# A two-layer hybrid block: norm weights spread by a product, a second layer's first weights split earlier, later transposes, another order at the end

## The chip, the cores and the metric

One core of a Trainium2 chip runs the kernel. It has five engines with their own instruction queues: TensorE (PE; its weight loads are PEld), VectorE (DVE), ScalarE (ACT), GpSimd (POOL) and SyncE (SP), which here issues transfers between HBM (DRAM) and the on-chip memory (SBUF). TensorE writes its sums to a second memory, PSUM. The metric is the device time of one execution in microseconds (us); the median of three runs is compared. The profile's span goes from the first to the last instruction of one execution.

## The reference

A sequence of 512 tokens with 1024 channels goes through two layers and a last norm. Each layer normalises, projects to the inputs of three mixers (an RWKV-7 recurrence, a gated linear recurrence, a latent attention of 8 heads), gates their outputs and adds their projection to the residual h.

```python
def rms_norm(x, g, eps=NORM_EPS):
    xf = x.astype(jnp.float32)
    y = xf * lax.rsqrt(jnp.mean(xf * xf, axis=-1, keepdims=True) + eps)
    return (y * g.astype(jnp.float32)).astype(x.dtype)

    h = x
    for l in range(DEPTH):
        xn = rms_norm(h, ln_g[l])
        proj = xn @ w_in[l]
        u_a, z_a, u_b, z_b, q_lat, kv_lat, k_rope, z_c = jnp.split(proj, pts, axis=-1)
        y_a = rwkv7_mix(u_a, ...)
        y_b = rms_norm(rglru_mix(u_b, ...), lru_out_g[l])
        y_c = rms_norm(mla_mix(q_lat, kv_lat, k_rope, ...), mla_out_g[l])
        y = jnp.concatenate([y_a * silu(z_a), y_b * silu(z_b), y_c * silu(z_c)], axis=-1)
        h = h + y @ w_out[l]
    return rms_norm(h, final_g)
```

The change touches the norms at the start of each layer, the first projections, and the last norm; not the mixers' arithmetic.

## The kernel before

**Tiling.** Tokens stand in four tiles of 128 (`tt` 0 to 3), channels in halves of 512 (`n`) or blocks of 128. The normalised input is kept transposed, channels on the partitions, as a pair: `xH`, rounded to the fast f32 form of TensorE, and `xL`, the rest. Weights are split likewise: `weights` (L216) loads a raw half of 128x512 into one of three buffers `wr`, ScalarE rounds it into one of four `wH` (L141, the line of every plain copy), and VectorE or POOL subtracts for `wL` (L229). A product takes three matmuls (`mm3`, L233 to L235): high by high, high by low, low by high.

**The opening.** SyncE's queue loads x tile by tile (L158), the identity, the norm weights broadcast to 128 partitions (`gb0`, L173), and the first raw weights, in the order of the string `LO` ("0ig12uw3yvcm": digits are tiles of x, i the identity, g the norm weights, u and w the two halves of projection 12, y the first half of projection 0). For each tile `h_half` squares and sums two halves on ScalarE (L242), `h_rstd` makes the scale (VectorE L246, a logarithm and an exponential on ScalarE L138, VectorE L254 to L256), and `norm_tile` scales the tile by it and the norm weights (VectorE L298), transposes blocks of 128 on TensorE (L303) and splits them into `xH` (ScalarE L141) and `xL` (VectorE L306). Two PSUM buffers `ps` take the transposes. `behind` and `BN` hold certain weight copies on ScalarE behind the copies of a tile.

**A layer.** `one_layer` starts with projection 12 and projection 0, each in two halves of tokens (`halves=True`), so the first half needs tiles 0 and 1 only, the second tiles 2 and 3. Then come the other projections and the three mixers, in orders written out as strings. The attention's last step is `heads(3, ...)` (L1067 on): per block of keys it transposes the probabilities (L1076), copies them (L141), and multiplies them with the values (L1084), with products of the first output projection (`units`) in between.

**The passage to the next layer.** `out_proj(2, ..., True)` adds the attention's part of the output projection. For channel half `n` = 1 it works tile after tile: residual load `hp` (L446), 12 matmuls, `finish`. `finish` adds the residual (VectorE L461), writes h back (L464), squares (L242), multiplies with the norm weights (`norm_gain`, L286, POOL for n = 0, VectorE for n = 1), and at n = 1 calls `norm_tile`, which there scales what `norm_gain` left (L301), transposes and splits. After the second layer it calls `final_tile` instead: scale, VectorE for n = 1 (L316), ScalarE for n = 0 (L141), and one transfer out for each half (L319), from SyncE's and ScalarE's queues.

**Order.** The source gives each engine's instructions in program order; the builder then puts them into each engine's queue, so the order in a trace isn't that of the source. `tc.issue_after(i)` keeps the instructions of a block behind `i` on `i`'s engine.

## Time and profile before

| | us |
|---|---|
| median of three runs (849.64 to 851.14) | 849.87 |
| the profiled execution | 847.71 |
| its span | 845.9 |
| TensorE busy in the span | 791.7 |
| VectorE, ScalarE, POOL busy | 538.9, 519.3, 353.3 |

Mean granted TensorE clock: 0.984. The span begins with loads; TensorE's first instruction starts at 9.28 us, the first product of a projection at 15.87. Layer two's first product starts at 430.31, the last product of the kernel at 836.81.

How to read the rows below. A row of the order of time has the start, the duration, engine, line, operation, output tile <- input tiles, the shape, xN for N merged instructions, and in brackets the engine's idle time before it with what ended it. A row of a stretch has start:end, its length, the busy time of PE, PEld, DVE, ACT and POOL with instruction counts, the granted clock (1.00 is full), the DMA engines' busy share, and GB/s. SPq and ACTq are transfers being issued. A row of the transfers has what is loaded, the queue, the count, the size and the median us from issue to landing.

### The profile page before, as it was taken

How to read it: one execution, taken by the hardware profiler on the slowest of the kernel's cores; microseconds unless marked ns; L12 is line 12 of the kernel's file. 1: busy time of each engine (PE TensorE's matmuls, PEld its weight loads, DVE VectorE, ACT ScalarE, POOL GpSimd, SP SyncE). 2: the span in 40 equal slices, each digit the busy share in tenths (PEclk: the TensorE clock that was granted, in tenths of full speed). 3: DMA queues.
4: the chain of work that ended last, by engine and by line, in shares of the span. 5: the costliest groups of instructions: out<-in, count | busy, mean ns of one | idle time of the engine just before them, and what ended most of it. 6: DMA issues, size and time to landing. Idle time of an engine off the chain costs nothing. (4 is left out here: it accounts for less than half of the span.)

```text
span 845.9 us, 15219 instructions
## 1 busy us (share of the span) xinstructions
PE 791.7 (94%) x5696; PEld 619.4 (73%) x5696; DVE 538.9 (64%) x1115; ACT 519.3 (61%) x1018; POOL 353.3 (42%) x321
## 2 busy tenths in 40 slices
PE   4999999999879999999989999999998799999995
PEld 3878888886659877657778788888765697775674
DVE  5678776924977364774474966695367953577636
ACT  5667875657563576664467687845666436765635
POOL 0455557522452455022344556574143425530323
PEclk9999999999998999999999999999999899999998
DMA  7222134311113375123732233332001234731354
GB/s 246 98 76 74 66 111 132 112 58 33 33 39 113 120 229 193 55 90 92 272 122 89 75 100 100 101 112 92 30 26 43 80 95 140 244 120 50 112 174 162
DMA packets 49754, 91.07 MB, mean 108 GB/s; under 512 B 5520, under 2 KB 8336, under 8 KB 49680
## 3 DMA queue, kind: packets, MB, share of 16 engines
q1 hardware_dynamic: 49104, 89.05, 32.8%
q8 instruction: 45, 0.74, 0.4%
q10 hardware_dynamic: 576, 1.05, 0.3%
q14 instruction: 29, 0.24, 0.1%
HBM read 73.30 MB, written 16.78 MB: 106 GB/s over the span
## 5 line engine op out<-in xcount | busy, mean ns | idle before, releaser
L229 POOL TENSOR_TENSOR wL<-wr,wH 128x512 fp32r<-128x512 f32 (+1 forms) x148 | 196.8, 1336 | 283.9 <-ACT wH L141 270.4
L141 ACT ACTIVATE wH<-wr 128x512 fp32r<-128x512 f32 (+1 forms) x192 | 118.8, 622 | 142.8 <-PE acc L234 73.9
L233 PE MATMUL acc<-xH,wH 128*128 128x512 f32 (+1 forms) x496 | 191.9, 388 | 0.0
L234 PE MATMUL acc<-xL,wH 128*128 128x512 f32 (+1 forms) x496 | 189.3, 382 | 0.7 <-DVE xL L306 0.6
L235 PE MATMUL acc<-xH,wL 128*128 128x512 f32 (+1 forms) x496 | 188.5, 380 | 0.0
L234 PEld LDWEIGHTS acc<-xL,wH 128*128 128x128 f32 x496 | 94.0, 190 | 17.5 <-DVE xL L306 1.4
L233 PEld LDWEIGHTS acc<-xH,wH 128*128 128x128 f32 x496 | 93.5, 189 | 18.1 <-ACT xH L141 0.7
L235 PEld LDWEIGHTS acc<-xH,wL 128*128 128x128 f32 x496 | 93.9, 189 | 17.2
L233 PE MATMUL acc<-wH,c 128*128 128x512 f32 x192 | 82.5, 430 | 0.1
L234 PE MATMUL acc<-wL,c 128*128 128x512 f32 x192 | 76.7, 399 | 0.0
L235 PE MATMUL acc<-wH,c 128*128 128x512 f32 x192 | 76.2, 397 | 0.0
L141 ACT ACTIVATE UV<-ps 64x512 f32<-64x512 f32 (+4 forms) x112 | 52.4, 494 | 28.8 <-PE ps L1076 22.0
L229 DVE TENSOR_TENSOR wL<-wr,wH 128x512 fp32r<-128x512 f32 (+1 forms) x44 | 32.6, 744 | 53.0 <-ACT wH L141 52.9
L138 ACT ACTIVATE c<-acc,sm 128x128 f32<-128x128 f32 (+3 forms) x64 | 33.6, 528 | 19.0 <-DVE sm L1060 19.0
L1058 PE MATMUL acc<-am,am 128*128 128x128 f32 (+3 forms) x128 | 42.8, 447 | 0.9 <-ACT c L138 0.8
L234 PEld LDWEIGHTS acc<-wL,c 128*128 128x128 f32 x192 | 36.5, 190 | 8.7 <-issue 1.9
L233 PEld LDWEIGHTS acc<-wH,c 128*128 128x128 f32 x192 | 36.3, 189 | 8.7 <-issue 2.2
L235 PEld LDWEIGHTS acc<-wH,c 128*128 128x128 f32 x192 | 36.3, 189 | 8.2 <-issue 0.5
L136 ACT ACT_TABLE_LOAD x31 | 39.8, 1283 | 1.3 <-PEq L1215 0.7
L138 ACT ACTIVATE g<-g 128x512 f32<-128x512 f32 (+1 forms) x58 | 36.4, 628 | 4.6 <-DVE g L705 2.6
L369 POOL TENSOR_TENSOR g<-g,g 128x512 f32<-128x512 f32 x24 | 32.2, 1340 | 13.9 <-ACT g L138 13.9
L141 ACT ACTIVATE c<-g 128x512 fp32r<-128x512 f32 (+1 forms) x40 | 24.9, 629 | 18.8 <-DVE g L980 7.2
(219 smaller groups left out, 1587.7 us busy)
## 6 DMA issues: line engine op xcount, KB each, us to landing
wr<-in_wc_dram SPq DMA_DIRECT2D x116, 256.0 KB, 2.7
wr<-in_wo_dram SPq DMA_DIRECT2D x48, 256.0 KB, 3.4
hp<-dr SPq DMA_DIRECT2D x38, 256.0 KB, 3.5
dr<-hp SPq DMA_DIRECT2D x28, 256.0 KB, 3.3
dr<-g SPq DMA_DIRECT2D x16, 256.0 KB, 2.5
g<-dr SPq DMA_DIRECT2D x16, 256.0 KB, 3.5
wr<-in_wl_dram SPq DMA_DIRECT2D x16, 208.0 KB, 2.5
dr<-c SPq DMA_DIRECT2D x12, 256.0 KB, 3.7
```

Of the source, the lines that this page charges most:

```text
L136: chained(A.preload_act_table_set(SETS[st]))
L138: chained(A.activation(out=out, in_=in_, func=func, **kw))
L141: i = A.activation(out=out, in_=in_, func=AF.Copy, **kw)
L229: (V if wn[0] % wmod[0] == 0 or wn[0] <= 4 else G).tensor_tensor(out=L, in0=raw, in1=f(H), op=ALU.subtract)
L233: PE.matmul(o, a[0], b[0], start=start, stop=False)
L234: PE.matmul(o, a[0], b[1], start=False, stop=False)
L235: PE.matmul(o, a[1], b[0], start=False, stop=stop)
L369: G.tensor_tensor(out=z, in0=z, in1=s, op=ALU.mult)
L1058: PE.matmul(o[:, 0:n], qT[:, hd, qt * 128:n], K2[:, p, e, 0:n], start=True, stop=True)
```

## The change

Four places are edited.

1. **Opening.** The identity and the norm weights are loaded from ScalarE's queue, the norm weights as a single row on one partition. Two matmuls with a row of ones (`on1`) spread this row over 128 partitions into the two PSUM banks `ck` (`go`), and the scaling reads its factor there. SyncE's order becomes 0, u, w, 1, 2, y, 3, v, c, m, kept by `issue_after(queued)`, with the small later loads (`w2a2`, `gagx`) behind it. `keep_warm` issues 3, 5 and 3 matmuls (128 x 256, plain f32, result unused) behind the two spreading matmuls and behind the transposes of tiles 0 and 1. The two halves of projection 12 are split right behind tile 0's steps (`wfirst`).
2. **Attention's last step of layer one.** `first_weights(1)` loads and splits the four halves of layer two's projections 12 and 0 there, into a tile of the tag `am` (two buffers, shared with the attention's keys and queries), subtracting on POOL. `proj` then takes them from `wfirst`.
3. **Passage between the layers.** `norm_tile` is divided into `norm_scale` (at each tile's `finish`) and `norm_transposes`; the transposes of tiles 0 and 1 are issued after `finish` of tiles 2 and 3, those of 2 and 3 at the end.
4. **End.** ScalarE's scalings of the last norm go behind the table-ordered activation issued last; tile 3's second half is scaled and multiplied by the norm weights in one VectorE step; the first half of tile 2 is scaled and written after tile 3's.

```diff
-    BN = (2, 2, 0, 0)
+    BN = (0, 2, 0, 0)
-    LO = "0ig12uw3yvcm"
+    LO = "gi0uw12y3vcm"
-    raws, gb0 = {}, c4([128, D])
+    raws, gb0, on1 = {}, c4([128, D]), g2([1, 128])
+    G.memset(on1, 1.0)
-        "i": lambda: nc.sync.dma_start(out=C[:, 0:128], in_=cst[:, 0:128]),
+        "i": lambda: nc.scalar.dma_start(out=C[:, 0:128], in_=cst[:, 0:128]),
-        "g": lambda: nc.sync.dma_start(out=gb0, in_=ln_g[0].partition_broadcast(128)),
+        "g": lambda: nc.scalar.dma_start(out=gb0[0:1, :], in_=ln_g[0].unsqueeze(0)),
+    queued = None
     for t in LO:
-        x_load(int(t)) if t.isdigit() else loads[t]()
+        with (tc.issue_after(queued) if queued is not None and t not in "gi" else nullcontext()):
+            i = x_load(int(t)) if t.isdigit() else loads[t]()
+        if t not in "gi":
+            queued = getattr(i, "ins", i)
...
+            scaled[0] = V.scalar_tensor_tensor(out=src, in0=h[tt][:, s], scalar=rs, in1=gb[j], op0=ALU.mult, op1=ALU.mult).ins
             for k in range(4):
-                PE.transpose(p[:, k, :], src[:, k * 128:(k + 1) * 128], ident)
+                warmed[0] = PE.transpose(p[:, k, :], src[:, k * 128:(k + 1) * 128], ident).ins
...
+    def keep_warm(o, n):
+        w = smask.rearrange("p c s -> p (c s)")
+        with tc.issue_after(warmed[0]):
+            for _ in range(n):
+                i = PE.matmul(o, w[:, 0:128], w[:, 0:256], start=True, stop=True).ins
+        warmed[0] = i
...
+    def norm_scale(tt):
+        rs = h_rstd(tt)
+        for j in range(2):
+            V.tensor_scalar(out=hg[tt, j], in0=hg[tt, j], scalar1=rs, scalar2=None, op0=ALU.mult)
+
+    def norm_transposes(l, tt):
+        xH, xL, _ = xn[l]
+        c = slice(tt * 128, (tt + 1) * 128)
+        for j in range(2):
+            p = ps([128, 4, 128])
+            for k in range(4):
+                PE.transpose(p[:, k, :], hg[tt, j][:, k * 128:(k + 1) * 128], ident)
+            xh = xH[:, 4 * j:4 * j + 4, c]
+            copy(xh, p)
+            V.tensor_tensor(out=xL[:, 4 * j:4 * j + 4, c], in0=p, in1=f(xh), op=ALU.subtract)
+
+    def first_weights(l):
+        W = tl("am", [128, 4, 2, 512], F32R, bufs=2)
+        for i, (j, hf) in enumerate(((12, 0), (12, 1), (0, 0), (0, 1))):
+            raw = tl("wr", [128, 512], F32, bufs=3)
+            nc.sync.dma_start(out=raw, in_=wc[l, j, :, 4 * hf:4 * hf + 4, :].rearrange("p k c -> p (k c)"))
+            split(raw, W[:, i, 0, :], W[:, i, 1, :], G)
+            wfirst[j, hf] = W[:, i, 0, :], W[:, i, 1, :]
...
     def final_tile(tt):
-        rs = h_rstd(tt)
-        for n in range(2):
-            y = hg[tt, n]
-            if n:
+        fin[tt] = rs = h_rstd(tt)
+        for t, n in {2: ((2, 1),), 3: ((3, 1), (3, 0), (2, 0))}.get(tt, ((tt, 0), (tt, 1))):
+            y = hg[t, n] if (t, n) != (3, 1) else g2()
+            if (t, n) == (3, 1):
+                V.scalar_tensor_tensor(out=y, in0=h[t][:, 512:1024], scalar=rs, in1=xn[depth][2][:, 512:1024], op0=ALU.mult, op1=ALU.mult)
+            elif n:
                 V.tensor_scalar(out=y, in0=y, scalar1=rs, scalar2=None, op0=ALU.mult)
             else:
-                copy(y, y, scale=rs)
+                with tc.issue_after(last[0]):
+                    copy(y, y, scale=fin[t])
...
-                            norm_tile(l + 1, tt) if l + 1 < depth else final_tile(tt)
+                            norm_scale(tt) if l + 1 < depth else final_tile(tt)
...
                         finish(tt)
+                        if tt >= 2 and l + 1 < depth:
+                            norm_transposes(l + 1, tt - 2)
+                    if l + 1 < depth:
+                        for tt in (2, 3):
+                            norm_transposes(l + 1, tt)
...
             if p < 3:
                 ahead += score_steps(p + 1)
+            elif l + 1 < depth:
+                first_weights(l + 1)
             heads(p, [lambda t=t: emit(t) for t in s.split(",")])
...
-    norm_start(0, gb0)
+    go, wk = [ck(), ck()], acc([128, 256])
+    for n in range(2):
+        warmed[0] = PE.matmul(go[n], on1, gb0[0:1, n * 512:(n + 1) * 512], start=True, stop=True).ins
+    norm_start(0, go)
+    keep_warm(wk, 3)
     for tt in range(4):
...
-        last_v = norm_tile(0, tt)
+        last_v = norm_first(tt)
+        if tt < 2:
+            keep_warm(wk, (5, 3)[tt])
+        if tt == 0:
+            behind += [last[0]] * 2
+            with tc.issue_after(scaled[0]):
+                wfirst.update({(12, hf): weights(None, raw=raws.pop((12, hf))) for hf in range(2)})
```

## The prediction

> **What bounds the kernel now.** I read the page's totals first, then the order of time at three places (the opening, the passage between the layers, the end), because the diff touches only these and the last attention step.

> ```profile
> span 845.9 us, 15219 instructions
> PE 791.7 (94%) x5696; PEld 619.4 (73%) x5696; DVE 538.9 (64%) x1115; ACT 519.3 (61%) x1018; POOL 353.3 (42%) x321
> ...
> 25.24:115.00 89.76, 87.92 (x470) 72.70 (x471) 63.20 (x78) 65.15 (x108) 48.25 (x53) 1.00 0.28 89
> ```

> TensorE is busy 94% of the span, and for the 90 us behind the opening 87.92 of 89.76 us. So a stretch in which it waits, if shortened, moves everything behind it forward by that much; work moved on another engine inside a full stretch moves nothing. The profiled execution took 847.71 us, 1.8 us around its span; the median of the three timed runs is 849.87. I work out differences on the profiled execution and take them from the median.

> The opening, in order of time, and its stretches (the five engines' busy times, clock, DMA share, GB/s):

> ```profile
> 3.46 0.63 ACT L242 ACTIVATE g<-c 128x512 f32<-128x512 f32 x1 [1.44 <-DMA c<-in_x_dram]
> ...
> 5.92 0.16 DVE L256 SCALAR_TENSOR_TENSOR sm<-sm,sm 128x1 f32<-128x1 f32 x1
> ...
> 8.47 1.42 DVE L298 SCALAR_TENSOR_TENSOR g<-c,sm,c 128x512 f32<-128x512 f32 x2 [2.39 <-DMA c<-in_ln_g_dram]
> ...
> 9.02 0.63 ACT L242 ACTIVATE g<-c 128x512 f32<-128x512 f32 x1 [3.52 <-DMA c<-in_x_dram]
> ...
> 12.60 0.69 DVE L229 TENSOR_TENSOR wL<-wr,wH 128x512 fp32r<-128x512 f32 x1
> ...
> 13.20 1.41 DVE L298 SCALAR_TENSOR_TENSOR g<-c,sm,c 128x512 f32<-128x512 f32 x2
> ...
> 14.10 1.94 PE L303 MATMUL ps<-C,g 128*128 128x128 f32 x8 [2.85 <-DVE g L298]
> ...
> 15.87 0.58 PE L233 MATMUL acc<-xH,wH 128*128 128x256 f32 x1
> ...
> 20.54 0.60 PE L303 MATMUL ps<-C,g 128*128 128x128 f32 x4
> ...
> 25.24 0.50 PE L233 MATMUL acc<-xH,wH 128*128 128x256 f32 x2
> ...
> 0.00:4.00 4.00, 0.00 (x0) 0.00 (x0) 0.00 (x0) 1.82 (x3) 0.93 (x10) 1.00 0.58 154
> 4.00:6.00 2.00, 0.00 (x0) 0.00 (x0) 0.56 (x4) 1.24 (x6) 0.00 (x0) 1.00 0.71 152
> 6.00:8.00 2.00, 0.00 (x0) 0.00 (x0) 0.08 (x1) 0.00 (x0) 0.00 (x0) 1.00 0.95 329
> 8.00:10.00 2.00, 0.72 (x4) 0.72 (x5) 1.42 (x2) 0.98 (x3) 0.00 (x0) 1.00 1.05 392
> ```

> Tile 0 of x is there at 3.46 and its scale at 6.08, but the scaling (L298) waits 2.39 us for the broadcast norm weights; tile 1 of x comes at 9.02, after ScalarE stood 3.52 us. While the broadcast is under way, from 4 to 6 us, the DMA moves only 152 GB/s at a share of 0.71. The first product waits for tiles 0 and 1 (15.87), the second half of that projection for tiles 2 and 3 (25.24). The opening is bound by its loads, then by the chain of norm steps on VectorE and ScalarE.

> **The opening, part by part.** The broadcast (512 KB) becomes one row of 4 KB, and leaves SyncE's queue with the identity; two products of one row spread it into PSUM. In the queue tile 1 of x now stands behind tile 0 and two weight halves: 0.52 + 0.26 + 0.26 + 0.52 = 1.57 MB, 1.64 with identity and row. Up to 4 us the DMA moved 0.62 MB (154 GB/s × 4 us); the other 1.02 MB at 329 GB/s take 3.1 us. Tile 1 lands at about 7.1 instead of 9.02, **−1.9**, and at the 392 GB/s that the next stretch reached, −2.4; I take −2.1. Tile 0's scaling can begin at 6.1 (−2.4) if the row is spread by then. That product is not in the trace. The row is issued first and x itself, issued at 0.74, was in use at 3.46, so it is there at 3.5 to 4.5. Half-clock products of 512 columns are seen between the layers:

> ```profile
> 426.24 0.63 PE L235 MATMUL acc<-wH,c 128*128 128x512 f32 x1
> ...
> 426.66 0.62 PE L233 MATMUL acc<-wH,c 128*128 128x512 f32 x1
> ...
> 390.89 1.72 PE L1084 MATMUL ck<-UV 128*64 128x512 f32 x8
> ```

> They start 0.42 us apart. Plain f32 takes two passes (the eight instructions of the L1084 row are four products of the source), so two rows take 4 × 0.42 = 1.7 us, and the three warming products of 256 columns 6 × 0.21 = 1.3: TensorE is done at 6.5 to 7.5, and the first transposes want it at 6.8. At most 0.7 us is lost there. At best it costs nothing.

> The scaling reads PSUM now; the nearest row of that kind (L461, quoted below) takes 0.75 for one half against 1.42 / 2 = 0.71: 8 × 0.04 = **+0.3**. The warming products cost nothing: they stand where TensorE idles (2.85 us before 14.10), at worst 0.7 us ahead of the first product, which then still ends before tile 3 is ready. They should make the second tile's eight transposes 2 × 0.60 instead of 1.94; the first half of that is on the chain, **−0.3**. The first weights' split is put right behind tile 0's scaling, so the 0.69 us at 12.60 no longer stands ahead of tile 1's scaling: **−0.7**; it is 0 if it only comes in tile 0's way. The copies stand behind tile 0's exponential on ScalarE, in its former gap. No other VectorE work is taken from tiles 2 and 3, so the gain is carried as it is to tile 3 and the product at 25.24: −2.1 + 0.3 − 0.3 − 0.7 = **−2.8**, bounds −0.7 and −4.0.

> **Between the layers.** Stretches, then TensorE, VectorE, POOL and SyncE's queue:

> ```profile
> 421.50:431.20 9.70, 5.32 (x25) 4.12 (x24) 9.51 (x21) 6.52 (x17) 5.13 (x6) 0.82 0.44 159
> ...
> 424.04 1.97 PE L303 MATMUL ps<-C,g 128*128 128x128 f32 x8 [2.49 <-DVE g L301]
> ...
> 428.77 0.66 PE L303 MATMUL ps<-C,g 128*128 128x128 f32 x4 [1.01 <-DVE xL L306]
> ...
> 429.93 0.63 PE L303 MATMUL ps<-C,g 128*128 128x128 f32 x4 [0.51 <-DVE sm L254]
> ...
> 431.17 0.39 PE L234 MATMUL acc<-xL,wH 128*128 128x256 f32 x1 [0.37 <-DVE xL L306]
> ...
> 418.53 0.75 DVE L461 SCALAR_TENSOR_TENSOR c<-acc,sm,hp 128x512 f32<-128x512 f32 x1 [1.84 <-DMA hp<-dr]
> ...
> 424.30 1.27 DVE L254 TENSOR_TENSOR sm<-sm 128x1 f32<-128x1 f32 x1
> ...
> 426.09 1.24 DVE L255 SCALAR_TENSOR_TENSOR sm<-sm,sm 128x1 f32<-128x1 f32 x1
> ...
> 434.22 0.16 DVE L255 SCALAR_TENSOR_TENSOR sm<-sm,sm 128x1 f32<-128x1 f32 x1
> ...
> 423.93 3.38 POOL L229 TENSOR_TENSOR wL<-wr,wH 128x512 fp32r<-128x512 f32 x2
> ...
> 409.74 2.45 SPq L221 DMA_DIRECT2D wr<-in_wc_dram  x2
> ```

> Here 2.49 + 1.01 + 0.51 + 0.37 = 4.4 us of TensorE are idle, and the clock is 0.82. But VectorE is busy 9.51 of 9.70 us: it is the bound, from a late load of the residual (418.53) on. The diff takes no instruction from VectorE here. Moving transposes later in the program does little by itself: tile 0's transposes already stand in the source right behind tile 0's products and yet ran at 424.04, behind most of tile 3's, so the order on an engine goes by what is ready when it is built, and they are ready no sooner. The four split weight halves do go, but three buffers for raw weights and four for split ones then hold the next four: the loads at 409.74 and the POOL splits at 423.93 come back under another name, and SyncE's queue and its waits stay. I take **0**, bounds +1.5 (the second half of the split of x, L306, now ranks behind tile 3's steps) and −4.4.

> The splits' new place, the last attention step:

> ```profile
> 385.00:390.00 5.00, 5.00 (x34) 3.86 (x34) 1.94 (x3) 3.33 (x8) 1.29 (x1) 1.00 0.31 105
> ...
> 393.08 0.66 ACT L141 ACTIVATE UV<-ps 128x256 f32<-128x256 f32 x2 [3.54 <-PE ps L1076]
> ...
> 397.00 3.00 POOL L229 TENSOR_TENSOR wL<-wr,wH 128x512 fp32r<-128x512 f32 x2 [8.43 <-ACT wH L141]
> ...
> wr<-in_wo_dram SPq DMA_DIRECT2D x6, 256.0 KB, 4.2
> ```

> Four copies of 0.63 as at 3.46 (2.5 us on ScalarE) and four subtractions of 3.00 / 2 = 1.5 (6.0 on POOL) fit into the gaps of 3.54 and 8.43 us; four loads of 256 KB meet a DMA share of 0.31. **0**, bounds 0 and +6.5 (rival 2).

> **The end.**

> ```profile
> 839.06 0.69 DVE L286 TENSOR_TENSOR g<-c,c 128x512 f32<-128x512 f32 x1
> ...
> 839.92 0.20 ACT L138 ACTIVATE sm<-sm 128x1 f32<-128x1 f32 x1 [0.34 <-DVE sm L246]
> ...
> 840.11 0.72 ACT L141 ACTIVATE g<-g,sm 128x512 f32<-128x512 f32 x1
> ...
> 840.95 0.20 ACT L138 ACTIVATE sm<-sm 128x1 f32<-128x1 f32 x1
> ...
> 841.83 0.72 ACT L141 ACTIVATE g<-g,sm 128x512 f32<-128x512 f32 x1 [0.68 <-DVE sm L256]
> ```

> Tile 2's copy (840.11, 0.72) stands between tile 3's logarithm and its exponential. It moves behind the exponential, into the 0.7 us in which VectorE finishes tile 3's scale: the exponential runs at 840.0 to 840.2. VectorE loses L286 (0.69) ahead of tile 3's scale. With the exponential's end at 840.2 instead of 841.15, tile 3's copy ends 0.9 us sooner than 842.55, at 841.65: **−0.9**; −0.2 if tile 2's copy comes last. The output transfers behind it stay.

> Sum: −2.8 + 0 + 0 − 0.9 = −3.7, and 849.87 − 3.7 = **846.2**.

> **Rivals.** 1. *The passage shrinks too.* The two small VectorE steps at 424.30 and 426.09 take 1.27 and 1.24 instead of 0.16 while POOL splits weights: 2.2 us. If the next weights are not split just there, the first product of layer two comes 2.2 us sooner: 846.2 − 2.2 = **844.0**. For it: the splits named in the diff are those at 423.93; against it: the next four are ready at the same time. [...] Chance 0.20.

> 2. *The early split stalls attention.* The fourth raw half needs a buffer that POOL frees after 1.5 us, and its load then takes 4.2. If ScalarE's copy of it is queued ahead of the copies that feed the probabilities to TensorE, these stand 5.7 us, and TensorE, once its other products run out, idles and restarts at half clock (0.8 us, as the eight transposes at 424.04 took 1.97 instead of 2 × 0.60): up to 6.5, 846.2 + 6.5 = **852.7**. It decides from a stall of 3.7 us on. Against it: TensorE has output products to fill with, ScalarE 3.54 us of slack. Chance 0.07.

> 3. *Tile 1 comes no sooner.* The two weight halves that now go ahead of it are 0.52 MB, as much as the broadcast was. If the engines gave the broadcast no more than its bytes, tile 1 still lands at 9.02 and only −0.7 is left: 849.87 − 0.7 − 0.9 = **848.3**. Against it stands the 152 GB/s between 4 and 6 us. [...] Chance 0.15.

> **How the numbers follow.** My forecast has 0.55, with 844.8 to 847.6 of its own (opening −2 to −4, passage ±0.7); 0.03 is left for a changed order elsewhere. A measurement of this kernel tells about 0.2%, 1.7 us, from no change. Rival 3 is within that; rival 2 above; so faster 0.78, same 0.15, slower 0.07. The range takes in rival 1 with some of the passage's bound and rival 3: 843.0 to 848.6.

> **What would show it.** Right: the first L233 product of the first projection near 13.3 instead of 15.87, its second half near 22.4 instead of 25.24, tile 1's square near 7; unchanged gaps of about 4.4 us between the layers, with POOL splits still beside the small VectorE steps; tile 3's exponential right behind its logarithm and the span's end 0.9 us nearer to the last product. Wrong: a square of tile 1 still near 9, an idle TensorE in the last attention step, or a passage with a clock of 1.00.

## The result, and the profile after

| | median, us | runs | ratio to before [95%] |
|---|---|---|---|
| before | 849.75 (848.39 to 851.14) | 4 | |
| after | 856.33 (855.39 to 857.87) | 4 | 1.0079 [1.0057, 1.0101] |

The change makes the kernel slower by 6.6 us, where 3.7 us less had been forecast. The profiled execution of the changed kernel took 856.30 us, with a span of 854.5 and a mean granted clock of 0.978 (before: 0.984). The profiled execution of the kernel before, 847.71 us, lay 2 us below its median, so the two traces differ by 8.6 us, not by 6.6.

The page of the changed kernel, first its totals:

```profile
span 854.5 us, 15271 instructions
PE 806.2 (94%) x5722; PEld 629.5 (74%) x5722; DVE 545.6 (64%) x1113; ACT 518.8 (61%) x1018; POOL 354.9 (42%) x323
```

TensorE is busy 14.5 us more, with 26 instructions more. These are the spreading and warming products of the opening, and they take 3.75 + 2.93 + 2.43 + 1.46 = 10.6 us, most of which it idled before. So the totals don't locate the loss. To find the place, the start of the same product is compared between the two traces (after minus before): second half of the first projection −1.13 us; first product of layer two +0.41; head sums of the first head pair in layer two +1.35 (460.49 against 459.14); the same of the second head pair (L525 before, L575 after) +3.29; of the next pair, 30 us later in the changed kernel, +9.32; last product +8.14. Nearly all is lost between 475 and 510 us, in layer two's first mixer, a stretch that the diff doesn't edit.

VectorE in that stretch, in order of time, in the kernel before and then in the changed one:

```profile
472.82 0.74 DVE L499 SCALAR_TENSOR_TENSOR g<-acc,omu,hp 128x512 f32<-128x512 f32 x1
473.48 1.11 DVE L593 SCALAR_TENSOR_TENSOR g<-g,vecs,g 128x512 f32<-128x512 f32 x1
```

```profile
474.61 1.58 DVE L643 SCALAR_TENSOR_TENSOR g<-g,vecs,g 128x512 f32<-128x512 f32 x1
476.12 0.74 DVE L548 SCALAR_TENSOR_TENSOR g<-acc,omu,hp 128x512 f32<-128x512 f32 x1
```

Two steps have changed places. The mix of `k` (L499, now L548) feeds the next head sums; the bonus step (L593, now L643) is wanted by nobody soon. Before, the mix came first. TensorE at these head sums, before and after, with the stretches (columns: busy time of PE, PEld, DVE, ACT, POOL, then the clock):

```profile
475.41 0.50 PE L525 MATMUL ps<-c,bones 128*128 128x512 f32 x1 [0.55 <-ACT c L141]
476.49 0.50 PE L526 MATMUL ps<-c,bones 128*128 128x512 f32 x1 [0.59 <-DVE c L211]
...
480.00:490.00 10.00, 10.00 (x50) 8.28 (x50) 9.35 (x15) 8.24 (x15) 3.43 (x6) 1.00 0.18 53
```

```profile
478.70 0.80 PE L575 MATMUL ps<-c,bones 128*128 128x512 f32 x1 [2.49 <-ACT c L141]
480.08 0.80 PE L576 MATMUL ps<-c,bones 128*128 128x512 f32 x1 [0.58 <-DVE c L217]
...
480.00:490.00 10.00, 9.92 (x44) 7.82 (x45) 5.55 (x10) 5.79 (x10) 1.36 (x2) 0.50 0.17 54
```

The wait grows from 0.55 to 2.49 us, and behind it the granted clock is 0.50, for the whole of 480 to 492 us, while TensorE is busy for 11.92 of these 12 us. In this stretch products of 128x512 start 0.43 us apart (from 490.36 on), behind it 0.23 (from 492.35 on). By estimate twelve us at half clock are six lost: 3.3 + 6.0 = 9.3, the shift that the next pair's head sums show.

The opening, TensorE and then the other two engines:

```profile
2.56 3.75 PE L1176 MATMUL ck<-c,g 1*128 1x512 f32 x4 [2.56 <-DMA c<-in_ln_g_dram]
6.24 2.93 PE L318 MATMUL acc<-smask 128*128 128x256 f32 x6
8.96 1.91 PE L305 MATMUL ps<-C,g 128*128 128x128 f32 x8
10.67 2.43 PE L318 MATMUL acc<-smask 128*128 128x256 f32 x10
13.61 1.29 PE L305 MATMUL ps<-C,g 128*128 128x128 f32 x8 [0.52 <-DVE g L303]
14.73 1.46 PE L318 MATMUL acc<-smask 128*128 128x256 f32 x6
15.85 0.47 PE L239 MATMUL acc<-xH,wH 128*128 128x256 f32 x1
...
24.11 0.51 PE L239 MATMUL acc<-xH,wH 128*128 128x256 f32 x2
...
7.81 0.63 ACT L248 ACTIVATE g<-c 128x512 f32<-128x512 f32 x1 [0.50 <-DMA c<-in_x_dram]
...
6.40 1.41 DVE L303 SCALAR_TENSOR_TENSOR g<-c,sm,ck 128x512 f32<-128x512 f32 x2
...
10.69 0.69 DVE L308 TENSOR_TENSOR xL<-ps,xH 128x512 fp32r<-128x512 f32 x1 [1.68 <-ACT xH L141]
11.30 0.15 DVE L252 SCALAR_TENSOR_TENSOR sm<-sm 128x1 f32<-128x1 f32 x1
...
12.72 1.41 DVE L303 SCALAR_TENSOR_TENSOR g<-c,sm,ck 128x512 f32<-128x512 f32 x2
```

Tile 0 is scaled at 6.40 (8.47 before), but its transposes start only at 8.96: the six instructions of the warming products stand in front. Tile 1 is squared by 9.2 us, yet the first step of its scale (L252) is queued on VectorE behind the split of tile 0's transposes (L308 at 10.69) and runs at 11.30. So 2 us gained at tile 0 shrink to 0.5 us at tile 1's scaling (12.72 against 13.20) and to nothing at the first product (15.85 against 15.87); the second half, which doesn't depend on tile 0, keeps 1.13. In this pair of executions 1.1 us still stand at 252 us (a product at 252.46 instead of 253.56), and none at 262 (261.83 against 261.80); between them both traces have the clock at 0.50 over nearly the same time (253.2 to 260.1 and 253.1 to 259.9).

The passage between the layers, TensorE, VectorE and POOL:

```profile
423.60 1.74 PE L334 MATMUL ps<-C,g 128*128 128x128 f32 x8 [3.07 <-DVE g L326]
428.72 0.66 PE L334 MATMUL ps<-C,g 128*128 128x128 f32 x4 [1.27 <-DVE xL L337]
430.30 0.76 PE L334 MATMUL ps<-C,g 128*128 128x128 f32 x4 [0.93 <-DVE xL L337]
431.70 0.58 PE L240 MATMUL acc<-xL,am 128*128 128x256 f32 x1 [0.20 <-DVE xL L337]
...
423.86 1.27 DVE L260 TENSOR_TENSOR sm<-sm 128x1 f32<-128x1 f32 x1
425.65 1.24 DVE L261 SCALAR_TENSOR_TENSOR sm<-sm,sm 128x1 f32<-128x1 f32 x1
...
423.49 3.38 POOL L235 TENSOR_TENSOR wL<-wr,wH 128x512 fp32r<-128x512 f32 x2
```

TensorE idles 3.07 + 1.27 + 0.93 + 0.20 = 5.5 us instead of 4.4. POOL still splits weights here, the next four, and VectorE's small steps still take 1.27 and 1.24 us beside it.

The end, ScalarE and VectorE:

```profile
848.36 0.34 ACTq L362 DMA_DIRECT2D out_dram<-g  x1
848.74 0.44 ACT L138 ACTIVATE sm<-sm 128x1 f32<-128x1 f32 x2 [0.90 <-DVE sm L252]
849.09 1.49 ACT L141 ACTIVATE g<-g,sm 128x512 f32<-128x512 f32 x2
...
847.84 0.49 DVE L358 TENSOR_SCALAR g<-g,sm 128x512 f32<-128x512 f32 x1
848.24 0.15 DVE L252 SCALAR_TENSOR_TENSOR sm<-sm 128x1 f32<-128x1 f32 x1
```

Logarithm and exponential now follow each other (the two at 848.74), as forecast, but they come 0.90 us behind the last square. L252, which they need, stands behind tile 2's scaling on VectorE and is done at 848.39; then ScalarE itself still issues tile 2's transfer (848.36, 0.34). Both tiles' copies (849.09, x2) end at 850.58, together with VectorE's last step (L356, done at 850.63): 5.7 us behind the start of the last product, as before (842.55 against 836.81).

### The profile page after: what moved, and what is told of

Read it like the earlier page. It is cut to its first block, busy times and chain, and to the rows that moved or that the text cites. A ratio compares the mean times of both kernels' runs of the same rounds, so it can differ in the third digit from the quotient of the medians.

```text
span 854.5 us, 15271 instructions
## 1 busy us (share of the span) xinstructions
PE 806.2 (94%) x5722; PEld 629.5 (74%) x5722; DVE 545.6 (64%) x1113; ACT 518.8 (61%) x1018; POOL 354.9 (42%) x323
## 5 line engine op out<-in xcount | busy, mean ns | idle before, releaser
L235 POOL TENSOR_TENSOR wL<-wr,wH 128x512 fp32r<-128x512 f32 (+1 forms) x145 | 193.3, 1339 | 297.7 <-ACT wH L141 279.0
L141 ACT ACTIVATE wH<-wr 128x512 fp32r<-128x512 f32 (+1 forms) x188 | 116.1, 622 | 143.5 <-PE acc L240 75.8
L239 PE MATMUL acc<-xH,wH 128*128 128x512 f32 (+1 forms) x464 | 183.5, 396 | 0.0
L240 PE MATMUL acc<-xL,wH 128*128 128x512 f32 (+1 forms) x464 | 180.2, 388 | 0.2 <-DVE xL L308 0.2
L241 PE MATMUL acc<-xH,wL 128*128 128x512 f32 (+1 forms) x464 | 180.1, 388 | 0.0
L239 PEld LDWEIGHTS acc<-xH,wH 128*128 128x128 f32 x464 | 87.8, 189 | 17.9 <-ACT xH L141 0.3
L241 PEld LDWEIGHTS acc<-xH,wL 128*128 128x128 f32 x464 | 87.8, 189 | 17.2
L240 PEld LDWEIGHTS acc<-xL,wH 128*128 128x128 f32 x464 | 88.0, 190 | 16.6 <-DVE xL L308 0.4
L141 ACT ACTIVATE UV<-ps 64x512 f32<-64x512 f32 (+4 forms) x112 | 52.4, 494 | 28.2 <-PE ps L1127 21.4
L235 DVE TENSOR_TENSOR wL<-wr,wH 128x512 fp32r<-128x512 f32 (+1 forms) x43 | 35.0, 820 | 51.8 <-ACT wH L141 51.7
L138 ACT ACTIVATE c<-acc,sm 128x128 f32<-128x128 f32 (+3 forms) x64 | 33.6, 528 | 17.8 <-DVE sm L1111 17.6
L138 ACT ACTIVATE g<-g 128x512 f32<-128x512 f32 (+1 forms) x58 | 36.4, 628 | 4.9 <-DVE g L756 2.6
L141 ACT ACTIVATE c<-g 128x512 fp32r<-128x512 f32 (+1 forms) x40 | 25.0, 629 | 19.4 <-DVE g L1031 7.9
## 6 DMA issues: line engine op xcount, KB each, us to landing
wr<-in_wc_dram SPq DMA_DIRECT2D x116, 256.0 KB, 2.6
wr<-in_wo_dram SPq DMA_DIRECT2D x48, 256.0 KB, 3.3
hp<-dr SPq DMA_DIRECT2D x38, 256.0 KB, 3.7
dr<-hp SPq DMA_DIRECT2D x28, 256.0 KB, 3.5
dr<-g SPq DMA_DIRECT2D x16, 256.0 KB, 2.4
g<-dr SPq DMA_DIRECT2D x16, 256.0 KB, 3.2
dr<-c SPq DMA_DIRECT2D x12, 256.0 KB, 3.8
```

Of the source, the lines that this page charges most:

```text
L138: chained(A.activation(out=out, in_=in_, func=func, **kw))
L141: i = A.activation(out=out, in_=in_, func=AF.Copy, **kw)
L235: (V if wn[0] % wmod[0] == 0 or wn[0] <= 4 else G).tensor_tensor(out=L, in0=raw, in1=f(H), op=ALU.subtract)
L239: PE.matmul(o, a[0], b[0], start=start, stop=False)
L240: PE.matmul(o, a[0], b[1], start=False, stop=False)
L241: PE.matmul(o, a[1], b[0], start=False, stop=stop)
```

## The experiments

All times are medians of several rounds beside the kernel before on the same chip; ratios are to that kernel, formed from all runs of both, and so not quite those of the medians. Filler products are extra work whose result nobody reads; nothing else of the computation is left out or added.

### What the swapped steps and the half clock are worth

The first kernel holds the bonus step behind the mix (`mixins[5]`). In the diff of each run the first line names the kernel that it starts from, and "..." stands for lines not shown.

```diff
 after
...
-            V.scalar_tensor_tensor(out=bo, in0=r, scalar=vc("r_k", p), in1=k, op0=ALU.mult, op1=ALU.mult)
+            with (tc.issue_after(mixins[5]) if p == 0 else nullcontext()):
+                V.scalar_tensor_tensor(out=bo, in0=r, scalar=vc("r_k", p), in1=k, op0=ALU.mult, op1=ALU.mult)
```

> The changed kernel with one order held: on VectorE the bonus step of head pair 0 (L643) stays behind the mix of k of head pair 1 (L548), as in the kernel before. Theory A (this swap opens the 2.49 us wait of TensorE in layer two and the half clock behind it, 9.32 - 1.35 = 8.0 us of shift): 856.3 - 8.0 = 848.3 us, clock 1.00 behind 478 us. Rival B (the later passage between the layers, not the swap, lets the clock fall): 855 or more, and the half clock stays.

Measured: 852.60 us, 1.0044 [1.0021, 1.0067]. Nearly half of the loss is gone. TensorE still waits 0.78 + 0.56 us and its clock is 0.50 from 478 to 488.

Without the early weights:

```diff
 after
-            elif l + 1 < depth:
-                first_weights(l + 1)
```

> The changed kernel without the split of layer two's first weights in the attention's last step; its built order has the bonus step behind the mix again. Theory A: the split matters only through the order, so the same 848.3 us as with the order held, within 1 us. Rival C (the split itself costs time in the attention step or the passage): 1 to 3 us less than the kernel with the order held, 845 to 847. Rival B: 855.

Measured: 849.54, 1.0006 [0.9992, 1.0021]. Without this part of the change the whole loss is gone. The waits are 0.55 + 0.58 and the clock is 1.00 again from 470 to 530 us.

The swap alone, in the kernel before (a dependency puts the mix behind the bonus step, layer two only):

```diff
 before
...
-            V.scalar_tensor_tensor(out=bo, in0=r, scalar=vc("r_k", p), in1=k, op0=ALU.mult, op1=ALU.mult)
+            i = V.scalar_tensor_tensor(out=bo, in0=r, scalar=vc("r_k", p), in1=k, op0=ALU.mult, op1=ALU.mult).ins
+            if l == 1 and p == 0:
+                tc.add_manual_dep(mixins[5], i.name, NOSYNC, reason="issue order")
```

> The kernel before with only those two VectorE steps swapped in layer two. Theory A: 849.8 + 8.0 = 857.8 us, with an idle TensorE of some 2.5 us near 475 us and a clock of 0.5 behind it. Rival B: the step's own 1.1 to 1.6 us at most, 849.8 to 851.4.

Measured: 852.75, 1.0047 [1.0028, 1.0067]: two VectorE steps in the other order cost 4.0 us by the ratio (0.0047 × 849.5). The wait is 1.86 + 0.54 us, the clock 0.50 from 480 to 488.

The changed kernel with products that keep TensorE busy while it waits:

```diff
 after
...
             o = ps()
+            if fill is not None:
+                w = smask.rearrange("p c s -> p (c s)")
+                with tc.issue_after(fill):
+                    for _ in range(10):
+                        PE.matmul(o[:, 0:256], w[:, 0:128], w[:, 0:256], start=True, stop=True)
             PE.matmul(o, bones, H, start=True, stop=False)
```

> The changed kernel, order as it is, with ten unused products of 128x256 put into TensorE's queue just ahead of the late head sums of pair 1 in layer two (about 2.5 us at full clock). Theory A1 (of the 8 us about 2 are the wait and 6 the half clock behind it): the clock stays at 1.00, 856.3 - 6 = 850.3 us. Rival A2 (the late step itself delays a chain, whatever the clock): 856 to 857.

Measured: 852.18, 1.0039 [1.0021, 1.0057]. The head sums start as late as in the changed kernel (478.88 against 478.70), but the clock stays at 1.00 from 470 to 530 us, and 0.0040 × 849.5 = 3.4 us come back. So the half clock behind the wait is a cost of its own. It is less than the six us worked out above: the next pair's head sums come 6.1 us sooner than in the changed kernel (503.02 against 509.12), the last product only 3.4 (841.51 against 844.95), so a part is lost again further on.

Both together, order held and three filler products:

```diff
 after, order held and with the filler
-                    for _ in range(10):
+                    for _ in range(3):
```

> The changed kernel with the bonus step of pair 0 held behind the mix of k of pair 1, and three unused 128x256 products (0.41 us each) ahead of the head sums of pair 1 in layer two. It tells apart what is left of the loss when the order is held (852.6, where TensorE still waited 0.8 + 0.6 us and its clock still fell to 0.5). Theory, the half clock behind that wait: the clock stays at 1.00 from 470 to 490 us, and the time is near 849.3. Rival, the early weights cost engine time of their own (their splits push ScalarE, GpSimd and VectorE back whatever the clock does): 851.5 to 852.5 with the clock up.

Measured: 852.26, 1.0039 [1.0023, 1.0055], no better than either. The rows say why, TensorE first:

```profile
476.17 0.49 PE L585 MATMUL ps<-c,bones 128*128 128x512 f32 x1 [0.32 <-DVE c L217]
...
479.21 1.13 PE L672 MATMUL ps<-c,c 64*128 64x128 f32 x8 [1.45 <-DVE c L623]
...
476.04 1.76 DVE L235 TENSOR_TENSOR wL<-wr,wH 128x512 fp32r<-128x512 f32 x1
477.73 0.74 DVE L552 SCALAR_TENSOR_TENSOR g<-acc,omu,hp 128x512 f32<-128x512 f32 x1
478.39 0.67 DVE L623 TENSOR_SCALAR c<-ps 128x512 f32<-128x512 f32 x1
```

The next products wait 1.45 us for L623, and in front of it on VectorE stands a *weight split* of 1.76 us. In the kernel before, POOL made two splits there, and VectorE's own came at other times:

```profile
475.88 2.93 POOL L229 TENSOR_TENSOR wL<-wr,wH 128x512 fp32r<-128x512 f32 x2
...
464.72 0.68 DVE L229 TENSOR_TENSOR wL<-wr,wH 128x512 fp32r<-128x512 f32 x1
485.18 0.69 DVE L229 TENSOR_TENSOR wL<-wr,wH 128x512 fp32r<-128x512 f32 x1
```

That leads to the cause.

### The cause: a counter

Which engine makes a split is decided by a running number in `weights`:

```python
        wn[0] += 1
        ...
        (V if wn[0] % wmod[0] == 0 or wn[0] <= 4 else G).tensor_tensor(out=L, in0=raw, in1=f(H), op=ALU.subtract)
```

In the mixers' projections every fifth goes to VectorE. `first_weights` makes four splits without calling `weights`, so in layer two the number is four lower, and another split of each five is VectorE's. With the number counted as before:

```diff
 after
             split(raw, W[:, i, 0, :], W[:, i, 1, :], G)
+            wn[0] += 1
             wfirst[j, hf] = W[:, i, 0, :], W[:, i, 1, :]
```

> The changed kernel, whose early weights now raise the counter by which weights() deals its splits (every fifth of the attention's to VectorE, the rest to GpSimd), as they did when they went through weights(). Theory, the whole loss comes from the deal being shifted by four in layer two: the mix of k of pair 1 comes ahead of the bonus step again, the splits of VectorE fall near 448, 464 and 485 us again, TensorE waits 0.5 + 0.6 us for the head sums of pair 1, its clock stays at 1.00 from 470 to 510 us, and the time is 847.0 to 849.5. Rival, the early split itself takes time from the attention's last step or the passage, whatever is dealt where: 851.5 to 853.0, as with the order held or the filler.

Measured: 850.01, 1.0005 [0.9991, 1.0018]. One line regains 0.0074 × 849.5 = 6.3 us. VectorE and TensorE in that run (its layer two starts 2.2 us later than in the profiled execution of before and is 4.3 us later at the first pair's head sums, 463.40 against 459.14, so all times are later):

```profile
477.10 0.74 DVE L549 SCALAR_TENSOR_TENSOR g<-acc,omu,hp 128x512 f32<-128x512 f32 x1
477.76 1.11 DVE L644 SCALAR_TENSOR_TENSOR g<-g,vecs,g 128x512 f32<-128x512 f32 x1
...
479.69 0.50 PE L576 MATMUL ps<-c,bones 128*128 128x512 f32 x1 [0.55 <-ACT c L141]
480.76 0.51 PE L577 MATMUL ps<-c,bones 128*128 128x512 f32 x1 [0.57 <-DVE c L217]
...
480.00:490.00 10.00, 9.39 (x62) 7.67 (x62) 8.93 (x14) 9.32 (x16) 4.31 (x7) 1.00 0.20 66
```

The mix stands ahead of the bonus step without being held there, and the clock is 1.00. Why the builder puts the two steps in the other order under the other deal isn't shown. The other way round, the kernel before with the number set back by four in layer two and nothing else:

```diff
 before
-            mix[p] = mixed(p, p == 0), mixed(4 + p), mixed(8 + p)
+            m = mixed(p, p == 0)
+            if (l, p) == (1, 0):
+                wn[0] -= 4
+            mix[p] = m, mixed(4 + p), mixed(8 + p)
```

> The kernel before, with that counter set back by four behind the first projections of layer two, and nothing else. Theory: the loss comes without any of the change's parts, 853.5 to 856.5, with the bonus step ahead of the mix, two waits at the head sums of pair 1 of about 2.5 + 0.6 us and a clock of 0.5 from 480 to 490 us. Rival, only the swapped steps count: 852.7 as in the run that swapped them. If the deal is harmless: 849.0.

Measured: 856.31, 1.0069 [1.0042, 1.0096], the changed kernel's time without any of its parts:

```profile
476.10 1.58 DVE L596 SCALAR_TENSOR_TENSOR g<-g,vecs,g 128x512 f32<-128x512 f32 x1
477.61 0.74 DVE L499 SCALAR_TENSOR_TENSOR g<-acc,omu,hp 128x512 f32<-128x512 f32 x1
...
480.19 0.79 PE L525 MATMUL ps<-c,bones 128*128 128x512 f32 x1 [2.48 <-ACT c L141]
...
480.00:490.00 10.00, 9.21 (x39) 6.84 (x39) 5.79 (x8) 6.91 (x12) 2.40 (x4) 0.51 0.16 54
```

Two more values of the number, on the opening alone (below), by the same edit with `+= 2` and `+= 3`:

> The opening alone (0.998 of the kernel before), with the counter of the deal advanced by two behind the first projections of layer two; in VectorE's queue the bonus step then stands ahead of the mix of k of pair 1 again. Theory, the phase of the deal decides by that order: 851.5 to 853.5 (ratio 1.003 to 1.005), a wait of 1.9 to 2.5 us at the head sums of pair 1 and a clock of 0.5 from 480 to 488 us. Rival, only the shift by four is harmful: 847.

Measured: 854.15, 1.0062 [1.0040, 1.0084]; bonus step first, a wait of 2.57 us, a clock of 0.50 from 480 to 490. The theory's price was a little low.

> The same with the counter advanced by three, where the mix stands ahead of the bonus step as in the kernel before. Theory: waits of 0.5 + 0.6 us, clock 1.00, 847 (ratio 0.998). Rival, a split of VectorE falls behind the head sums' subtraction, as in the run that held the order, and costs a wait of 0.8 us and the clock: 851 to 852.

Measured: 846.77, 0.9993 [0.9975, 1.0012], mix first. Neither account of the waits was right: they are 1.47 + 0.89 us, and still the clock is 1.00 from 470 to 500 us.

```profile
474.83 0.50 PE L565 MATMUL ps<-c,bones 128*128 128x512 f32 x1 [1.47 <-ACT c L141]
476.21 0.49 PE L566 MATMUL ps<-c,bones 128*128 128x512 f32 x1 [0.89 <-DVE c L217]
...
480.00:490.00 10.00, 10.00 (x49) 8.21 (x48) 9.32 (x11) 7.27 (x13) 4.37 (x5) 1.00 0.08 27
```

That was the profiled execution, 846.68 us. The twelve runs of this kernel lie in two groups, seven from 845.1 to 846.9 and five from 849.8 to 851.7. Their mean clocks, which are known for every run, are 0.989 and 0.984. A half clock of 8 us lowers the mean of 850 us by 0.5 × 8 / 850 = 0.0047, so by estimate the five had about 8 us more of it. Where is not shown, as only one of the seven was profiled. The kernel with the number set back by four does the same: three runs at 850.8 to 852.1 us with a mean clock of 0.984, six at 855.4 to 859.4 with 0.979.

### Opening, passage and end one by one

The changed kernel without early weights and with the transposes at each tile again:

```diff
 after, without first_weights
-                        if tt >= 2 and l + 1 < depth:
-                            norm_transposes(l + 1, tt - 2)
-                    if l + 1 < depth:
-                        for tt in (2, 3):
-                            norm_transposes(l + 1, tt)
+                        if l + 1 < depth:
+                            norm_transposes(l + 1, tt)
```

> The changed kernel without the early split and with the transposes of the norm at each tile again: the opening and the order at the end alone. Against the run without the early split (849.54). Theory, the late transposes lengthen the idle time between the layers (there 1.8 + 3.3 us against 4.4 in the kernel before): 848.6, with an idle stretch near 2.5 + 1.0 + 0.5 us. Rival, their place is free: 849.5.

Measured: 846.80, 0.9979 [0.9961, 0.9997].

The two kernels without early weights, each without its warming products:

```diff
 after, without first_weights (the second also with the transposes at each tile)
-    keep_warm(wk, 3)
...
-        if tt < 2:
-            keep_warm(wk, (5, 3)[tt])
```

> The changed kernel without the early split and without the warming products. Theory, the warming products stand ahead of tile 0's transposes and hold them from about 7.1 to 8.96 us, and what they gain in clock they lose in place: tile 0's transposes near 7.1, the first projection product between 14 and 15.9 us, second half by 23.5, time 848.5. Rival, they pay by the clock: transposes of tile 1 and the first products at half clock again, first product near 15.9, second half near 24.8, time 850.0.

Measured: 848.40, 0.9995 [0.9981, 1.0009].

> Only the opening without its warming products, and the order at the end: no early split, transposes at each tile. If both the late transposes and the warming products cost something, this is the fastest of the four, near 847.7; if neither does, all four lie within 849.0 to 850.0.

Measured: 848.41, 0.9993 [0.9972, 1.0013]. With late transposes the warming products seem to cost 1.1 us (849.54 against 848.40), with the transposes at each tile to gain 1.6 (846.80 against 848.41): opposite signs, both inside the intervals, so no verdict. The trace of the first shows both of the forecast's effects at once:

```profile
7.32 1.97 PE L305 MATMUL ps<-C,g 128*128 128x128 f32 x8 [1.19 <-DVE g L303]
12.39 1.94 PE L305 MATMUL ps<-C,g 128*128 128x128 f32 x8 [3.10 <-DVE g L303]
14.16 0.58 PE L239 MATMUL acc<-xH,wH 128*128 128x256 f32 x1
```

The first product comes 1.7 us sooner (14.16 against 15.85), but the products (128x256) start 0.21 us apart (15.27 to 16.34) instead of 0.12 in the changed kernel. 0.21 is also the pace of such products in the passage of the opening alone (430.96 to 433.95), where the profile's clock reads 0.50; in the opening it reads 1.00 (before and after, 0 to 30 us), so the pace is read from the starts. The second half comes at 24.78, no sooner than with warming (24.11 in the changed kernel).

The counted number (`wn[0] += 1`) with the transposes at each tile, then the opening alone: no early weights, transposes at each tile, and `final_tile` of the kernel before.

> As the run with the counter kept, and the transposes of the norm at each tile again. Theory, the early split with the deal kept takes four splits out of the passage and the transposes at each tile keep its idle time short: 846.0. Rival, the early split gains nothing there: 846.8, as the opening and the end alone gave.

Measured: 847.30, 0.9982 [0.9966, 0.9997]: the early split, dealt as before, gains nothing (846.80 without it).

> The kernel before with the new opening alone: no early split, transposes at each tile, end as before. Against the opening and the order at the end together (846.8). If the order at the end gains the 0.9 that was forecast: 847.7. If it gains nothing: 846.8. If it costs what the changed kernel's end showed (last product to span end 9.2 us against 8.7): 846.3.

Measured: 846.92, 0.9980 [0.9961, 1.0000]: the opening gains about 1.7 us, at the edge of what these runs can tell, and the new order at the end nothing.

The opening and the late transposes, the same kernel without the edit that puts them back to each tile:

> The opening and the transposes two tiles later: no early split, end as before. Against the opening alone (0.998 of the kernel before). Theory, the late transposes cost near 2.7 us: ratio 1.001, near 849.7. Rival, that difference was scatter: ratio 0.998, near 847.

Measured: 849.71, 1.0008 [0.9997, 1.0019]. The three pairs give 2.7, 2.7 and 2.8 us by the medians (2.0 to 2.4 by the ratios) for the late transposes, each difference uncertain by some 2 us. Filler products in the passage test whether that is the clock:

```diff
 after, counted; the opening alone; after, counted, with the transposes at each tile
             p = ps([128, 4, 128])
+            w = smask.rearrange("p c s -> p (c s)")
+            for _ in range({(0, 0): 6, (1, 0): 2, (1, 1): 1}.get((tt, j), 0)):
+                with tc.issue_after(lastmm[0]):
+                    PE.matmul(p[:, 0:2, :].rearrange("p a b -> p (a b)"), w[:, 0:128], w[:, 0:256], start=True, stop=True)
```

> The changed kernel with the counter kept, and nine unused 128x256 products (0.41 us each) in the passage: six ahead of tile 0's transposes, two and one ahead of tile 1's. Against 850.0 without them. Theory, the late transposes cost by the half clock behind their waits (0.50 to 0.53 from 432 to 438 us): the clock stays near 1.00 from 424 to 438 us, and the time is 847.5 to 848.0. Rival, VectorE's steps set the passage and the clock beside them is free: 849.5 to 850.0, with the clock up or not.

> The opening alone with the same nine products in the passage. There the clock was 0.50 from 424 to 434 us, and some 30 products at half clock cost 0.2 us each beside a full clock. Theory, clock: 844.5 to 845.5 (0.9945 of the kernel before). Rival, VectorE sets the passage: 846.9, or the products push tile 0's transposes back by up to 0.5 us: 847.4.

> The kernel with the counter kept and the transposes at each tile, with the same nine products in the passage. Against 847.3 without them. Theory, clock: 845.5. Rival, VectorE: 847.3. If the early split gains anything once the clock is held, this is below the opening alone with the products.

Measured: 850.08, 1.0004 [0.9993, 1.0015]; 848.75, 0.9998 [0.9987, 1.0008]; 849.61, 1.0004 [0.9993, 1.0016]. The first against 850.01 without the products: no change, though the clock is 1.00 from 428 to 438 us where it had been 0.50 to 0.53 in 432 to 438. The other two, with a clock of 1.00 from 418 to 438 us, are 1.5 and 1.9 us slower by the ratios than without. So a full clock in the passage gains nothing net of the products that hold it, which fits the reading that VectorE sets the passage. With these products in, late transposes and transposes at each tile also come out alike (1.0004 both), and the early split gains nothing (849.61 against 848.75). What exactly the late transposes cost without them stays open: the profiled executions of the last pair have spans of 847.0 (late) and 847.2 (at each tile) and don't show the difference; the latter was far above its kernel's median (849.06 us against 846.92).

## Why the prediction was wrong

**The step that failed: the attention's last step, put at 0 with bounds 0 and +6.5, and with it the premise that the diff touches only this step, the opening, the passage and the end.** Its four copies, subtractions and loads were weighed, and they cost nothing there, as forecast: with the number counted, the early split is worth −0.1 and +0.3 us (1.0005 against 1.0006, 0.9982 against 0.9979). What the step left out is that those four splits had passed through `weights`, and that their passing decided which engine makes every later split of layer two. That costs 6.3 us. It is none of the three rivals; it is the "changed order elsewhere" to which the prediction gave 0.03, without looking for one. Rival 2's stall of the attention didn't happen, and that its 852.7 lies on the side of the result is luck.

The other steps:

- **Opening, −2.8 (bounds −0.7 and −4.0).** Measured about −1.7 [−3.3, 0]: right in sign and within its bounds, too large. Tile 1's square came at 7.81, not near 7 (9.02 before), so −1.2 of the −2.1. Reading PSUM cost nothing instead of +0.3 (1.41 for the two steps, as 1.42 before). The warm transposes of tile 1 came as forecast (1.29 against 1.94). The failing term is "The warming products cost nothing", at worst 0.7 us: they held tile 0's transposes to 8.96, and through VectorE's queue the scale of tile 1. The sum gave the spreading 1.7 us and the first warming group 1.3; they took 3.75 and 2.93, as their instructions started some 0.85 and 0.43 us apart where the rows taken for them gave 0.42 and 0.21. The first product at 15.85 instead of 13.3, and the second half at 24.11 instead of 22.4, follow. Without the products the cost stands in the pace of the first products (0.21 us apart instead of 0.12).
- **Passage, 0 (bounds +1.5 and −4.4).** The reading was right: VectorE bounds it (busy for 10.09 of 10.20 us, 421.5 to 431.7), the POOL splits came back under another name, the slow small steps too, and rival 1 (844.0) did not come. But the late transposes cost 2.0 to 2.4 us by the ratios, above the bound, as far as differences uncertain by some 2 us tell.
- **End, −0.9.** Measured 0. The exponential did move next to the logarithm, but the logarithm was then the late one, behind tile 2's scaling on VectorE and tile 2's transfer on ScalarE, and tile 2's copy still came ahead of tile 3's last.
- **Rival 3** (tile 1 no sooner, 848.3) fell: 7.81 against 9.02.

By the ratios: −1.7 (opening) + 0 (end) + 2.4 (late transposes) + 0.1 (early split) + 6.3 (deal) = +7.1 us, against 0.0079 × 849.5 = +6.7 [4.8, 8.6] for the whole.

## What to carry to other kernels

Where a helper counts its calls and chooses an engine or a buffer by the count, a call that is added, moved or bypassed re-deals everything behind it; ask of each edit which counters, rotations and orders it shifts, and compare the built order of instructions in places that the edit doesn't touch. Behind a short TensorE wait read the granted clock too, not the wait alone: here a swap of two VectorE steps put the head sums back by 1.7 us and, with a clock of 0.50 from 480 to 488 us, the next pair's by 6.2 (477.08 against 475.41, 506.00 against 499.80), of which 4.0 are left in the time. The opening alone (846.92) or with the new order at the end (846.80, 0.9979 [0.9961, 0.9997]) is some 0.2% faster than the kernel before, and clearly faster than the changed one.

## What was not expected of the hardware

In five of the kernels in the table, and with the number set back by four, the granted clock fell to 0.50 behind short waits of TensorE and stayed there for 7 to 14 us, through products that hardly paused (in the changed kernel TensorE was busy for 11.92 of the 12 us from 480 to 492):

| kernel | waits around the head sums, us | clock 480 to 490 us |
|---|---|---|
| before | 0.55 + 0.59 | 1.00 |
| order held | 0.78 + 0.56 | 0.59 |
| order held, three filler products | 0.32 + 1.45 | 0.66 |
| number advanced by three | 1.47 + 0.89 | 1.00 |
| swap alone | 1.86 + 0.54 | 0.55 |
| after | 2.49 + 0.58 | 0.50 |
| number advanced by two | 2.57 + 0.31 | 0.50 |

TensorE was busy for 0.9 to 2.1 us in the steps before the falls at these head sums. How soon the clock came back differs too: in the kernel before it rose behind a single step at half clock with 3.11 us of busy TensorE (423.73 to 427.15), in the changed kernel two steps with TensorE busy throughout (481.92 to 488.75) went by at half clock, and it rose behind the next, at 492.16. Why it took so long here is open.
